# Rotary embedding on one core: three TensorE tiles instead of five, one store on another queue, the first batch's store cut into three

## The chip, the cores and the metric

The kernel runs on one core of a Trainium2 chip. The metric is device microseconds (us) of one execution of the whole program: it loads the input from HBM, rotates it and stores the result to HBM. The core has five engines with an instruction stream each (TensorE, PE in the profile; VectorE, DVE; ScalarE, ACT; GpSimd, POOL; SyncE, SP) and 16 DMA engines that do the transfers. In this kernel DMAs are started from two streams, SP and ACT, and each of the two has a DMA queue of its own: q1 is SP's and q10 is ACT's.

## The reference

`x` is 8 x 2048 x 8 x 64 in float32 (batch, position, head, element); `cos` and `sin` are 2048 x 32. Each half of a head is multiplied with both tables:

```python
x1 = x[..., : x.shape[-1] // 2]
x2 = x[..., x.shape[-1] // 2 :]
out1 = x1 * cos - x2 * sin
out2 = x1 * sin + x2 * cos
return np.concatenate([out1, out2], axis=-1)
```

Input and output are 33.55 MB each, so the work is two products and a sum for each element that is loaded once and stored once.

## The kernel before

**Tiling.** A batch is one tile `xt` of 128 partitions. Partition q holds 16 consecutive positions of 8 x 64 elements, that is 8192 floats, a row of 32 KB that is contiguous in HBM. So a whole batch is moved by one DMA of 128 rows of 32 KB (4 MB), 8 rows for each of the 16 DMA engines. Five such buffers exist (`NBUF`). The result is written over the input in the same tile and stored from there. Batches are numbered 0 to 7 here, as in the code; x3 is the load of batch 3 and s3 its store.

**Loads (SP, line 67).** At the start SP issues the first batch in three pieces of 8, 8 and 16 KB rows (x0), the cosine table after the first of them (line 69), and then x1 to x4. After the work on batch b the loop issues the load of batch b+5 (lines 184 to 193); it takes the buffer of batch b and so waits for that batch's store. These are x5, x6 and x7.

**Units and their three kinds (`rotate`, lines 102 to 168).** A batch is worked on in units of 2048 elements per partition, four to a batch (`UNIT`, 8 KB of a row). The first batch has two half units ahead of three whole ones, the last batch two half units at its end. `kinds` (lines 98 to 100) names those units, always the first of a batch, that do not go the ordinary way. I write (b,u) for unit u of batch b.

- Kind A, the ordinary one: POOL makes the sine product in two halves (line 122, into `t2`), DVE makes the cosine product (line 129, into `t1`, in PSUM, one buffer), and DVE adds the two into `xt` (line 136).
- Kind B: POOL makes the sine product and DVE the cosine product as in A, but TensorE adds them by multiplying both with an identity matrix into PSUM (lines 143 and 144), and ACT copies the sums into `xt` (line 145).
- Kind C: DVE makes both products (lines 129 and 148), TensorE adds them (lines 160 and 161), ACT copies (line 165). POOL does nothing.

So a unit of kind A costs DVE two passes, B one, C two; POOL has two halves to do in A and B, and none in C. Before the change (1,0) and (3,0) are C, (2,0), (4,0) and (5,0) are B, all others A. `t2` of kinds A and B has three buffers, `t1` of kind B and both products of kind C share two others (`t1s`), and the PSUM tile `o` of the sums has one buffer.

**Order.** Nearly all instructions are held in program order on their engine (`keep`). Each engine works through its own list: DVE unit by unit, POOL the same units ahead of it, as far as loads and the three buffers of `t2` allow.

**Stores (line 74).** A store is issued when the units it covers are done. `shares` (lines 177 to 182) gives the cuts: batch 0 in two stores of 16 KB rows, batches 1 to 6 in one store of 32 KB rows, batch 7 in stores of 16, 8 and 8 KB rows. Stores of batches 0 to 6 go out on ACT's stream, in between its copies; those of batch 7 on SP's.

Of the kernel before, what the change touches and what calls it, by code (L numbers as in the profile page):

```python
# [10 lines left out]
def kernel(  # L11
# [7 lines left out]
    nc = tc.nc  # L19
# [4 lines left out]
    B, S, H, D = x.shape  # L24
    Dh = D // 2
    P = 128
    HD = H * D
    R = S // P
    ROW = R * HD
    UNIT = 4 * HD  # L30
    NBUF = 5
    C = 512
    last = B - 1
# [36 lines left out]
        xts[b] = xt  # L70

    def store(b, lo, n):
        queue = nc.sync if b == last else nc.scalar
        keep(queue.dma_start(out=ov[b, :, lo : lo + n], in_=xts[b][:, lo : lo + n]))  # L74

    keep(nc.scalar.dma_start(out=sin_sb, in_=sin_src))
# [19 lines left out]
        return dataclasses.replace(a, ap=[a.ap[0][:], a.ap[1][:], [0, n], a.ap[-1][:]])  # L96

    kinds = {}
    for b, kind in ((1, "C"), (2, "B"), (3, "C"), (4, "B"), (5, "B")):
        kinds[(b, 0)] = kind  # L100

    def rotate(b, lo, n):
# [73 lines left out]

    def shares(b):
        if b == 0:
            return [2 * UNIT, 2 * UNIT]
        if b == last:  # L180
            return [2 * UNIT, UNIT, UNIT]
        return [ROW]

    for b in range(B):
        done = 0
        outs = list(spans(shares(b)))
        for lo, n in spans(pieces(b)):
            rotate(b, lo, n)
            done = lo + n
            while outs and sum(outs[0]) <= done:  # L190
                store(b, *outs.pop(0))
        if b + NBUF <= last:
            load(b + NBUF)
# [30 lines left out]
```

## Time and profile before

| what | value |
|---|---|
| three runs | 163.75, 163.81, 164.03 us, median 163.81 us |
| profiled execution | span 161.8 us from its first to its last instruction (161.82 unrounded) |
| DVE busy | 140.1 us, 87% of the span |
| POOL busy | 138.9 us, 86% |
| PE busy | 49.4 us, 31% |
| ACT busy | 12.8 us, 8% |
| time of the DMA packets, as a share of 16 engines' span | 55.5% on q1, 42.6% on q10 |
| HBM read, written | 34.08 MB, 33.55 MB |

The profile has no separate device time for the profiled execution; its span is all that it gives. The runs' median lies 2.0 us above the span, and these 2.0 us are what lies around the first and the last instruction. Times inside the profile count from the span's start. "Busy" counts an engine's own work and not the time in which it waits or issues DMAs. The trace also has a record of each DMA packet, with its queue, start, duration and size. In this kernel a packet is one row of a tile, so that a load of 128 rows is 128 packets, 8 for each DMA engine.

### The profile page before, as it was taken

The numbers are of one execution on the slowest core, as the hardware profiler recorded it, in microseconds if no ns is written. First come the engines' busy times: TensorE is split into PE (matmuls) and PEld (weight loads), VectorE is DVE, ScalarE is ACT, GpSimd is POOL, SyncE is SP. The second block draws the span as 40 slices with busy tenths as digits, with TensorE's granted clock in tenths as the row PEclk, the third lists the DMA queues.
The fourth block names the chain that finished last, engine by engine and source line by source line (L and its number), as shares of the span: only waits on it lengthen the run. The fifth ranks groups of instructions, "written<-read, shape, count | busy, mean of one in ns | idle before, by whom it ended". The sixth has DMA issues, their size and how long they took to land.

```text
span 161.8 us, 459 instructions
## 1 busy us (share of the span) xinstructions
PE 49.4 (31%) x80; PEld 18.5 (11%) x80; DVE 140.1 (87%) x66; ACT 12.8 (8%) x14; POOL 138.9 (86%) x70
## 2 busy tenths in 40 slices
PE   0000000597309760978049714972000000000000
PEld 0000000142004220322023301330000000000000
DVE  0297999999999999999999999199989999899950
ACT  3300000002200220021000220022000000000000
POOL 1399997998999999992999959999899997999800
PEclk9999999999975998589957995699655555555555
DMA  5999999999999999899899999999999999999995
GB/s 158 425 454 494 413 308 446 413 470 405 462 405 462 389 502 405 389 510 397 389 510 397 389 512 397 397 502 397 397 488 413 405 478 413 405 478 409 397 419 225
DMA packets 3314, 67.65 MB, mean 418 GB/s; under 512 B 368, under 2 KB 368, under 8 KB 624
## 3 DMA queue, kind: packets, MB, share of 16 engines
q1 hardware_dynamic: 2016, 38.01, 55.5%
q10 hardware_dynamic: 1296, 29.62, 42.6%
q14 instruction: 2, 0.02, 0.0%
HBM read 34.08 MB, written 33.55 MB: 418 GB/s over the span
## 4 chain that ended last, share of the span: by engine, by line
DMA 48%; DVE 37%; POOL 9%; issue 2%; DVEq 0%; SPq 0%; POOLq 0%; ACTq 0%
DMA xt<-in_x_dram 26%; DVE t L129 18%; DMA out_dram<-xt 18%; DVE xt L136 17%; POOL t L122 9%; DMA sin_sb<-in_sin_dram 4%; DVE t L148 1%; DVEq L136 0%; SPq L67 0%; POOLq L122 0%; ACTq L74 0%
## 5 line engine op out<-in xcount | busy, mean ns | idle before, releaser
L122 POOL TENSOR_TENSOR t<-xt,sin_sb 128x1024 f32<-128x1024 f32 (+1 forms) x32 | 70.4, 2199 | 13.5 <-DMA xt<-in_x_dram 8.3
L129 DVE TENSOR_TENSOR t<-xt,cos_ps 128x2048 f32<-128x2048 f32 (+1 forms) x34 | 73.4, 2167 | 0.8
L122 POOL TENSOR_TENSOR t<-xt,nsin 128x1024 f32<-128x1024 f32 (+1 forms) x32 | 70.3, 2196 | 0.0
L136 DVE TENSOR_TENSOR xt<-t,t 128x2048 f32<-128x2048 f32 (+1 forms) x29 | 62.2, 2145 | 8.2 <-POOL t L122 5.5
L143 PE MATMUL o<-t,eye 128*128 128x512 f32 x24 | 17.0, 799 | 23.1 <-DVE t L129 19.6
L160 PE MATMUL o<-t,eye 128*128 128x512 f32 x16 | 12.0, 844 | 37.8 <-DVE t L129 35.6
L144 PE MATMUL o<-t,eye 128*128 128x512 f32 x24 | 14.9, 709 | 0.0
L145 ACT COPY xt<-o 128x1024 f32<-128x1024 f32 x6 | 6.1, 1012 | 45.7 <-PE o L144 45.7
L143 PEld LDWEIGHTS o<-t,eye 128*128 128x128 f32 x24 | 5.5, 256 | 32.5 <-issue 26.5
L160 PEld LDWEIGHTS o<-t,eye 128*128 128x128 f32 x16 | 3.7, 256 | 43.2 <-issue 39.4
L165 ACT COPY xt<-o 128x1024 f32<-128x1024 f32 x4 | 4.0, 1012 | 47.8 <-PE o L161 47.8
L93 DVE COPY cos_ps<-cos_sb 128x512 f32<-128x512 f32 x1 | 0.7, 695 | 6.9 <-DMA cos_sb<-in_cos_dram 6.9
L144 PEld LDWEIGHTS o<-t,eye 128*128 128x128 f32 x24 | 5.6, 234 | 8.2 <-issue 7.6
L161 PE MATMUL o<-t,neye 128*128 128x512 f32 x8 | 6.3, 875 | 0.2
L148 DVE TENSOR_TENSOR t<-xt,sin_ps 128x2048 f32<-128x2048 f32 x2 | 4.6, 2281 | 0.0
L161 PE MATMUL o<-t,eye 128*128 128x512 f32 x8 | 4.1, 592 | 0.0
L161 PEld LDWEIGHTS o<-t,neye 128*128 128x128 f32 x8 | 2.2, 300 | 5.3 <-issue 3.6
L161 PEld LDWEIGHTS o<-t,eye 128*128 128x128 f32 x8 | 1.5, 190 | 1.9 <-issue 1.9
L90 ACT ACT_TABLE_LOAD x1 | 1.3, 1283 | 1.2 <-PEq L208 1.2
L90 ACT ACTIVATE nsin<-sin_sb 128x512 f32<-128x512 f32 x1 | 0.6, 629 | 4.0 <-DMA sin_sb<-in_sin_dram 4.0
L91 ACT COPY sin_ps<-sin_sb 128x512 f32<-128x512 f32 x1 | 0.6, 580 | 0.0
L80 POOL MEMSET eye<- 128x128 f32 x1 | 0.2, 204 | 0.3 <-POOLq L208 0.3
(6 smaller groups left out, 1.0 us busy)
## 6 DMA issues: line engine op xcount, KB each, us to landing
xt<-in_x_dram SPq DMA_DIRECT2D x7, 4096.0 KB, 42.8
out_dram<-xt ACTq DMA_DIRECT2D x6, 4096.0 KB, 27.2
out_dram<-xt ACTq DMA_DIRECT2D x2, 2048.0 KB, 22.3
xt<-in_x_dram SPq DMA_DIRECT2D x2, 1024.0 KB, 6.7
xt<-in_x_dram SPq DMA_DIRECT2D x1, 2048.0 KB, 12.2
out_dram<-xt SPq DMA_DIRECT2D x1, 2048.0 KB, 9.9
out_dram<-xt SPq DMA_DIRECT2D x2, 1024.0 KB, 6.2
sin_sb<-in_sin_dram ACTq DMA_DIRECT2D x1, 256.0 KB, 5.7
```

The costliest lines, as they stand in the source:

```text
L90: keep(nc.scalar.mul(nsin, sin_sb, -1.0))
L93: keep(nc.vector.tensor_copy(cos_ps, cos_sb))
L122: nc.gpsimd.tensor_mul(out=t2u[:, :, u, :].rearrange("p (r h) d -> p r h d", h=H), in0=xu[:, :, 1 - u, :].rearrange("p (r h) d -> p r h d" ...
L129: nc.vector.tensor_mul(out=t1.rearrange("p (r k d) -> p r k d", r=nr, d=Dh), in0=xk, in1=rep(cos_ps[:, r0 : r0 + nr, :], 2 * H),)
L136: keep(nc.vector.tensor_add(out=xt, in0=t1, in1=t2))
L143: nc.tensor.matmul(oc, eye, t1[:, cs], start=True, stop=False)
L144: nc.tensor.matmul(oc, eye, t2[:, cs], start=False, stop=True)
L145: keep(nc.scalar.copy(xt[:, 2 * j * C : 2 * (j + 1) * C], o))
L148: nc.vector.tensor_mul(out=t2.rearrange("p (r k d) -> p r k d", r=nr, d=Dh), in0=xk, in1=rep(sin_ps[:, r0 : r0 + nr, :], 2 * H),)
L160: nc.tensor.matmul(oc, eye, t1u[:, gs, u, :], start=True, stop=False)
L161: nc.tensor.matmul(oc, eye if u else neye, t2u[:, gs, 1 - u, :], start=False, stop=True)
L165: nc.scalar.copy(xu[:, :, u, :], o.rearrange("p (g d) -> p g d", d=Dh))
```

## The change

Three edits, and nothing else:

```diff
     def store(b, lo, n):
-        queue = nc.sync if b == last else nc.scalar
+        queue = nc.sync if b in (last, B - NBUF) else nc.scalar
         keep(queue.dma_start(out=ov[b, :, lo : lo + n], in_=xts[b][:, lo : lo + n]))
...
-    for b, kind in ((1, "C"), (2, "B"), (3, "C"), (4, "B"), (5, "B")):
+    for b, kind in ((1, "B"), (3, "C"), (5, "B")):
         kinds[(b, 0)] = kind
...
         if b == 0:
-            return [2 * UNIT, 2 * UNIT]
+            return [2 * HD, UNIT + 2 * HD, 2 * UNIT]
```

The first edit puts s3 (batch 3 = `B - NBUF`) on SP's stream. In program order the last load, x7, is issued right after batch 2, so s3 stands behind x7 on SP and on q1. The second makes (1,0) a B where it was a C, and (2,0) and (4,0) ordinary A units; (3,0) stays C and (5,0) stays B. The third cuts the store of batch 0 into rows of 4, 12 and 16 KB: the first part can go out when the first half unit is done, the second after the third piece, the last after the fifth.

## The prediction

> **What bounds the kernel now.** I began with the page's head, slices and queues.
>
> ```profile
> span 161.8 us, 459 instructions
> ...
> DMA  5999999999999999899899999999999999999995
> ...
> q1 hardware_dynamic: 2016, 38.01, 55.5%
> q10 hardware_dynamic: 1296, 29.62, 42.6%
> ```
>
> The packets of both queues fill 98.1% of 16 engines' span. By the packet records the first packet starts at 1.76 us and the last ends at 160.55; the packets' durations sum to 158.68 us per engine. So the DMA engines are never idle between their first and last packet, and no edit here takes a byte away. Next, the two busy engines' waits and DVE's timeline:
>
> ```profile
> POOL t L122 <- DMA xt<-in_x_dram: 8.3, 6, 3.0
> ...
> DVE xt L136 <- POOL t L122: 5.5, 4, 3.6
> ```
>
> ```profile
> 27.69 2.28 DVE L129 TENSOR_TENSOR t<-xt,cos_ps 128x2048 f32<-128x2048 f32 x1
> 29.88 2.28 DVE L148 TENSOR_TENSOR t<-xt,sin_ps 128x2048 f32<-128x2048 f32 x1
> 32.08 2.29 DVE L129 TENSOR_TENSOR t<-xt,cos_ps 128x2048 f32<-128x2048 f32 x1
> 34.48 2.29 DVE L136 TENSOR_TENSOR xt<-t,t 128x2048 f32<-128x2048 f32 x1
> 36.80 2.30 DVE L129 TENSOR_TENSOR t<-xt,cos_ps 128x2048 f32<-128x2048 f32 x1
> ...
> 105.13 2.29 DVE L136 TENSOR_TENSOR xt<-t,t 128x2048 f32<-128x2048 f32 x1 [3.57 <-POOL t L122]
> ...
> 119.66 2.29 DVE L136 TENSOR_TENSOR xt<-t,t 128x2048 f32<-128x2048 f32 x1 [0.46 <-POOL t L122]
> ...
> 139.09 2.29 DVE L136 TENSOR_TENSOR xt<-t,t 128x2048 f32<-128x2048 f32 x1 [0.64 <-POOL t L122]
> ...
> 154.79 1.23 DVE L136 TENSOR_TENSOR xt<-t,t 128x1024 f32<-128x1024 f32 x1
> ```
>
> DVE runs back to back; its waits for POOL are 5.5 us in four places. It ends at 156.02, the last 1 MB store is issued, its first packet starts at 157.43, just as the 8 KB store before it drains (last packet 157.73). So two bounds meet at the end: DMA work and the DVE chain. Less DVE work gains nothing, more is paid.
>
> **What a unit costs DVE.** From starts in the rows above: A is 4.72 us (32.08 to 36.80), C is 4.39 (27.69 to 32.08). B is one pass, 2.19 (the spacing of the passes at 27.69 and 29.88). An A directly before a B or C is 4.61 (57.77 to 62.38). A unit's second pass starts 2.40 after its first. POOL's half unit takes 2.29 to the next one, a unit 4.58.
>
> **Edit 1, three TensorE tiles.** (1,0) turns from C to B: DVE loses 2.20 and POOL gains 4.58 there. (2,0) and (4,0) turn from B to A: each costs DVE 4.72 - 2.19, and 0.11 because the A before loses its short end, 2.64. POOL's work there is unchanged. PE loses 32 of its 80 matmuls, and ACT four copies of 1.01; both engines wait most of the time, so this is worth nothing.
>
> The first cost is where POOL is late:
>
> ```profile
> 26.04 2.33 POOL L122 TENSOR_TENSOR t<-xt,sin_sb 128x1024 f32<-128x1024 f32 x1 [0.93 <-DMA xt<-in_x_dram]
> ...
> 32.92 2.33 POOL L122 TENSOR_TENSOR t<-xt,nsin 128x1024 f32<-128x1024 f32 x1
> ```
>
> POOL starts batch 1 when x1 lands, S = 26.04. Its first four halves end at 35.25. Before, these were (1,1) and (1,2), and C kept DVE busy meanwhile. After, they are (1,0) and (1,1). DVE would be ready to add (1,1) at 27.69 + 2.19 + 2.40 = 32.28, but can start only at S + 9.24. From there DVE has 4.72 per unit against POOL's 4.58 and stays the later one.
>
> From the add of (1,1) to DVE's end before: 156.02 - 34.48 = 121.54. Subtract the three waits above, less the ordinary gap of 0.10 in each: 3.46 + 0.36 + 0.53 = 4.35. They go because DVE arrives later than POOL: DVE starts batch 5 at about 103 instead of 97.07, while x5 need not be later. Add 2 x 2.64 = 5.28. The chain is **122.47 us**, and DVE ends at S + 9.24 + 122.47 = S + 131.71. With S = 26.04 that is 157.75, already 1.73 later than now.
>
> A new wait must be ruled out: `t2` has three buffers, and a B holds its buffer until TensorE has read it. Before, PE read (2,0)'s until 59.3 and POOL started (2,3) at 54.36 without a wait, in another buffer. If (1,3) should get (1,0)'s buffer, PE (10.8 us per B tile, from about 30.1) frees it at 40.9; POOL wants it at S + 13.7. That costs 0 to 1 us, and nothing from S = 27.2 on.
>
> **Edit 3, the first store in three.** Packet durations are 0.084 us for 2 KB, 0.309 for 8, 0.611 for 16, 1.213 for 32. In a straight line a row of 4 KB is 0.16 and one of 12 KB 0.46, an estimate from these. Batch 0's store is then 8 x (0.16 + 0.46 + 0.61) = 9.84 per engine against 9.78: nothing. But it starts earlier. The first part is ready at 10.26 (DVE's first add ends there), 8 us before the present first store, and ACT has nothing else to do. Its packets alternate row for row with x0's and x1's: x2 beside 16 KB rows took 14.1 us, near 8 x (1.213 + 0.611); x5 beside 32 KB rows 18.4, near 16 x 1.213. So all 8 of its rows go ahead of x1's end (1.27 us), and, since the second part is ready at 18.36 and queued behind, 0 to 3 rows of 12 KB (I take 1.5, 0.69). Now 0.76 us of store packets per engine go ahead of it. x1 lands 1.20 later.
>
> Against this stands a slow stretch:
>
> ```profile
> 20.00:24.00 4.00, 0.00 (x0) 0.00 (x0) 3.86 (x3) 0.00 (x0) 4.00 (x3) 1.00 0.91 303
> 24.00:94.00 70.00, 39.59 (x64) 14.77 (x64) 68.48 (x31) 7.30 (x8) 65.34 (x29) 0.85 1.00 432
> ```
>
> The last column is GB/s. x1's rows took up to 2.09 us there, 0.84 us per engine in excess, while nothing was stored; with the first store packets it ends. Whether stores in between prevent it no row says: 0 to 0.84, I take half. S = 26.04 + 1.20 - 0.42 = 26.82, with ends 25.71 (no 12 KB row, no slow stretch) and 27.93 (three rows, all of it).
>
> **Edit 2, s3 on SP.** On SP it is queued behind x7, whose issue waits for s2 (at 91.4 now); behind it stand only batch 7's stores from about 148. No load waits for s3, since batch 8 does not exist. After s2 the ACT queue is empty until s4 is ready near 104, so x6 and x7 get all engines (9.7 us per batch instead of 18.4). x7 lands near 115 instead of 134.3; s3 follows beside s4. That removes POOL's waits for x6 and x7 (0.76 and 1.14), but DVE is by then 2.5 us later than now and would not have felt them. Worth 0. DMA stays fed: without s5 its work lasts to about 131, and s5 is ready near 120.
>
> **The sum.** DVE ends at 26.82 + 131.71 = 158.5, against 156.02. From there to the span's end it is 5.8 us now; I take 5.6, because the last store no longer meets the one before it (some engines finished it 0.5 late), bounds 5.3 to 5.8. By then the other DMA work is done (160.5 less the last store's 2.5 is 158.0, and its first packet needs 1.4 from issue). Span 164.1; with the 2.0 that the median lies above the span, **166.1 us**, 1.4% slower. Own range: 25.71 + 131.71 + 5.3 + 2.0 = 164.7, and 27.93 + 131.71 + 5.8 + 2.0 = 167.4.
>
> **Rivals.**
> - *DMA stays the bound*: the wait at (1,1) fails to appear or is taken back, so that DVE ends at 156.02 + 5.28 - 2.20 - 4.35 = 154.8 and the last packet still ends at 160.55: 163.8. For it speaks the full DMA row; against it that POOL's two units after x1 need 9.2 us whoever waits. The Trainium skill ("DMA: Bandwidth & Descriptors", Where 436 GB/s comes from) puts the fabric's ceiling at 435.2 GB/s; the 432 above agrees with it, and by that rule alone the time would not move. 7%.
> - *Faster*: the slow stretch between 20 and 24 us is a matter of reading only, and the early 4 KB rows end it. DMA work is then 0.84 shorter: 163.0. It decides only if DVE ends before about 155.2, so it needs the first rival's condition too. 3%.
> - *A held buffer*: POOL's (5,3) gets the `t2` buffer of (5,0). PE then frees it only near 118, POOL ends at 122.8, and DVE, ready near 119, waits 3.7 more: 169.8. None of the three B tiles before did it. 5%.
> - *A queue is served in bulk*: an engine takes all 8 rows of a store before it changes queue. Then 8 x (0.16 + 0.46) = 4.96 goes ahead of x1, S is 29.8, the time 169.1. The Trainium skill (the same page, Queues, rings and completion order) says that a DMA engine changes its queue only after a packet, typically of 9 to 17 descriptors. Against it: from 22.7 to 23.2 us sixteen rows of x1 start between the first and the second row of the first store. 3%.
>
> **Chances.** The forecast 82%, the rivals as given. A measurement of this kernel can tell about 0.2%, 0.33 us, from no change. Slower: 82 + 5 + 3 = 90%; same 7%; faster 3%. The range 164.7 to 167.4 is the forecast's own, which its unknown costs make, and leaves the rivals' 18% out.
>
> **What will show it.** Right: DVE's first wait after 16 us stands at the add of (1,1), near 36, about 3.8 long, and none of the waits at 105, 119 and 139 is left; DVE ends near 158.5; x7 lands before 120; the DMA row has a gap ahead of the last store. Wrong: x1 landing outside 25.7 to 28, a wait of DVE for POOL in batches 5 to 7, or DVE done by 156.

## The result, and the profile after

The changed kernel takes 164.32 us (median of 4 runs, 164.25 to 164.40), the kernel before 163.78 (4 runs, among them the three listed above). The ratio is **1.0038, with a 95% interval of 1.0024 to 1.0052**: slower by 0.54 us. The direction is the forecast's. The size is not: 2.3 us were forecast, and 164.32 lies below the range of 164.7 to 167.4. The profiled execution of the changed kernel took 164.31 us, 1.8 more than its span.

The same rows of the page as before:

```profile
span 162.5 us, 388 instructions
...
DMA  5999999899999999999989999999999999999966
...
q1 hardware_dynamic: 2160, 42.21, 61.1%
q10 hardware_dynamic: 1296, 25.43, 36.6%
```

The last two slices of the DMA row read 66 where they read 95. The engines now run dry once, near the end. s3 shows in the queues: 4 MB have gone from q10 to q1. By the packet records x7's last packet ends at 116.9 us (132.6 before) and x7 lands at 118.6 (134.3), so s3's place did what it should.

DVE's waits and its own timeline (start, duration, engine, line, operation; in brackets the idle time ahead of it and what ended it):

```profile
DVE xt L136 <- POOL t L122: 3.7, 2, 2.9
```

```profile
27.89 4.48 DVE L129 TENSOR_TENSOR t<-xt,cos_ps 128x2048 f32<-128x2048 f32 x2
35.24 2.29 DVE L136 TENSOR_TENSOR xt<-t,t 128x2048 f32<-128x2048 f32 x1 [2.87 <-POOL t L122]
37.57 2.29 DVE L129 TENSOR_TENSOR t<-xt,cos_ps 128x2048 f32<-128x2048 f32 x1
...
107.72 2.29 DVE L136 TENSOR_TENSOR xt<-t,t 128x2048 f32<-128x2048 f32 x1
...
122.00 2.29 DVE L136 TENSOR_TENSOR xt<-t,t 128x2048 f32<-128x2048 f32 x1 [0.20 <-DVE t L129]
...
140.89 2.29 DVE L136 TENSOR_TENSOR xt<-t,t 128x2048 f32<-128x2048 f32 x1
...
156.59 1.23 DVE L136 TENSOR_TENSOR xt<-t,t 128x1024 f32<-128x1024 f32 x1
```

The new wait stands at the add of (1,1), as forecast; the three later ones (now at the rows of 107.72, 122.00 and 140.89) are gone or down to 0.20. DVE ends at 157.82, 1.80 later than before. POOL's first unit of batch 1 starts where it did before:

```profile
26.04 2.32 POOL L122 TENSOR_TENSOR t<-xt,sin_sb 128x1024 f32<-128x1024 f32 x1 [0.70 <-DMA xt<-in_x_dram]
```

So S is 26.04, and S plus the forecast's 131.71 gives 157.75 against the measured 157.82. The chain of DVE was right to 0.07 us. What lies behind it was not. These are the DMA engines from 156 to 160 us (each row of a tile counts in the slice in which it starts), first of the kernel before, then of the changed one: 40 slices of 0.1 us, and the one DMA issued in this window with its median time from issue to landing.

```profile
DMA  7999599599799599599599399379579579779322
...
out_dram<-xt SPq DMA_DIRECT2D x1, 1024.0 KB, 4.9
```

```profile
DMA  5995995992790590020000000099199359519709
...
out_dram<-xt SPq DMA_DIRECT2D x1, 1024.0 KB, 3.9
```

Before, the last store is issued at 156.05 into a queue that is still busy with the one before it, and takes 4.9 us to land. After, it is issued at 157.84, when hardly a row is left to start (one slice of 2 at 157.7, zeros from 157.8 to 158.6), and takes 3.9. DVE's end came 1.8 later, the end of the program 0.7.

### The profile page after: what moved, and what is told of

The parts are those of the page before. It is cut to its first block, busy times and chain, and to the rows that moved or that the text cites. A ratio compares the mean times of both kernels' runs of the same rounds, so it can differ in the third digit from the quotient of the medians.

```text
span 162.5 us, 388 instructions
## 1 busy us (share of the span) xinstructions
PE 30.9 (19%) x48; PEld 11.6 (7%) x48; DVE 142.9 (88%) x67; ACT 8.7 (5%) x10; POOL 143.2 (88%) x72
## 5 line engine op out<-in xcount | busy, mean ns | idle before, releaser
L122 POOL TENSOR_TENSOR t<-xt,sin_sb 128x1024 f32<-128x1024 f32 (+1 forms) x33 | 73.0, 2211 | 8.0 <-DMA sin_sb<-in_sin_dram 5.4
L122 POOL TENSOR_TENSOR t<-xt,nsin 128x1024 f32<-128x1024 f32 (+1 forms) x33 | 73.0, 2211 | 0.0
L136 DVE TENSOR_TENSOR xt<-t,t 128x2048 f32<-128x2048 f32 (+1 forms) x31 | 66.8, 2154 | 6.8 <-POOL t L122 3.7
L143 PE MATMUL o<-t,eye 128*128 128x512 f32 x16 | 12.2, 856 | 58.5 <-DVE t L129 56.2
L160 PE MATMUL o<-t,eye 128*128 128x512 f32 x8 | 6.0, 846 | 27.5 <-DVE t L129 26.4
L144 PE MATMUL o<-t,eye 128*128 128x512 f32 x16 | 10.6, 749 | 0.0
L143 PEld LDWEIGHTS o<-t,eye 128*128 128x128 f32 x16 | 3.7, 256 | 64.3 <-issue 60.0
L145 ACT COPY xt<-o 128x1024 f32<-128x1024 f32 x4 | 4.0, 1012 | 68.0 <-PE o L144 68.0
L144 PEld LDWEIGHTS o<-t,eye 128*128 128x128 f32 x16 | 4.2, 264 | 6.0 <-issue 6.0
L160 PEld LDWEIGHTS o<-t,eye 128*128 128x128 f32 x8 | 1.9, 257 | 30.7 <-issue 28.7
L165 ACT COPY xt<-o 128x1024 f32<-128x1024 f32 x2 | 2.0, 1012 | 35.9 <-PE o L161 35.9
L161 PE MATMUL o<-t,neye 128*128 128x512 f32 x4 | 3.1, 867 | 0.1
L148 DVE TENSOR_TENSOR t<-xt,sin_ps 128x2048 f32<-128x2048 f32 x1 | 2.3, 2280 | 0.0
L161 PE MATMUL o<-t,eye 128*128 128x512 f32 x4 | 2.0, 592 | 0.0
L161 PEld LDWEIGHTS o<-t,neye 128*128 128x128 f32 x4 | 1.0, 289 | 2.6 <-DVE t L148 1.6
L161 PEld LDWEIGHTS o<-t,eye 128*128 128x128 f32 x4 | 0.8, 190 | 1.0 <-issue 1.0
```

The costliest lines, as they stand in the source:

```text
L122: nc.gpsimd.tensor_mul(out=t2u[:, :, u, :].rearrange("p (r h) d -> p r h d", h=H), in0=xu[:, :, 1 - u, :].rearrange("p (r h) d -> p r h d" ...
L136: keep(nc.vector.tensor_add(out=xt, in0=t1, in1=t2))
L143: nc.tensor.matmul(oc, eye, t1[:, cs], start=True, stop=False)
L144: nc.tensor.matmul(oc, eye, t2[:, cs], start=False, stop=True)
L145: keep(nc.scalar.copy(xt[:, 2 * j * C : 2 * (j + 1) * C], o))
L148: nc.vector.tensor_mul(out=t2.rearrange("p (r k d) -> p r k d", r=nr, d=Dh), in0=xk, in1=rep(sin_ps[:, r0 : r0 + nr, :], 2 * H),)
```

## The experiments

The edits are numbered as in the prediction: edit 1 changes the kinds, edit 2 the queue of s3, edit 3 the cut of the first store. Ratios are against the kernel before, measured beside each experiment, where its median was 163.62 or 163.63 us.

**Theory 1**: two bounds, of which the later counts. DMA work ends the span near 161.8 whatever DVE does; DVE's end plus the last store on an idle queue, about 4.7 us, is the other. Before the change DVE had some 1.1 us of slack. **Theory 2** is the forecast's: the end follows DVE from the first microsecond, by 5.3 to 5.8 us, and something else in the change took time back. **Theory 3**: the cost comes from the new rows or the new queue, not from the kinds.

### Each edit alone

`kinds_only`, edit 1 alone:

```diff
-    for b, kind in ((1, "C"), (2, "B"), (3, "C"), (4, "B"), (5, "B")):
+    for b, kind in ((1, "B"), (3, "C"), (5, "B")):
```

> The kernel before with edit 1 alone: (1,0) as B, (2,0) and (4,0) as A; s3 and the first store as they were. Theory 1 (the end is the later of two bounds, DMA work, which ends the kernel at about 163.8 us, and the end of DVE plus about 4.7 us of last store plus 2.0; so DVE has about 1.1 us of slack before): DVE ends near 157.8, 1.8 later than before, of which 0.7 shows: 164.3 to 164.6 us, the whole of the change's cost. Theory 2 (the forecast's: the end always follows DVE by 5.3 to 5.8 us, and the early 4 KB rows or the moved store take something back): without the two other edits the time is at least 165.2. Theory 3 (the cost comes from the smaller rows or from s3's place, and the kinds are hidden): 163.8.

Measured: 164.47 us, ratio 1.0048 (1.0036 to 1.0060). DVE ends at 157.91, POOL starts batch 1 at 26.13. This lies where theory 1 put it (164.3 to 164.6) and is the change's whole cost, its interval overlapping the change's own; nothing in the two other edits is needed to explain it, and they take back nothing that shows.

`cut_only`, edit 3 alone:

```diff
-            return [2 * UNIT, 2 * UNIT]
+            return [2 * HD, UNIT + 2 * HD, 2 * UNIT]
```

> The kernel before with edit 3 alone: the first batch's store in rows of 4, 12 and 16 KB. Theory 1: DMA work is the same, DVE's end too; 163.6 to 164.0 us, within 0.2% of before. Theory 2: x1 lands up to 0.8 us later and that is made up by DVE's later waits; 163.8 as well, but POOL's first unit of batch 1 starts at 26.5 or later. Theory 3: about 164.3. In the packet records the slow rows of x1 between 20 and 24 us, 0.84 us per engine, are either gone (they belonged to reading alone) or there.

Measured: 163.42 us, 0.9996 (0.9985 to 1.0008). POOL's first unit of batch 1 starts at 26.10: x1 is not late. Its slow rows are gone, but the excess of all packets over the usual (median) duration of their size is 1.62 us per engine, against 1.56 before; it is now spread over many rows from 20 us on. DVE ends at 154.45, 1.6 earlier, where I had expected no change: x5 lands at 93.6 instead of 95.8, and the wait at (5,1) falls from 3.57 to 1.48.

`s3_only`, edit 2 alone:

```diff
-        queue = nc.sync if b == last else nc.scalar
+        queue = nc.sync if b in (last, B - NBUF) else nc.scalar
```

> The kernel before with edit 2 alone: s3 on SP, behind x7. Theories 1 and 2: x6 and x7 land earlier (x7 well before 125 instead of 134), DVE's waits at 119 and 139 us go, DVE ends about 0.9 earlier, and the time stays at 163.8, since DMA work is the bound; within 0.2%. Theory 3: above 164.1, because DMA runs dry somewhere once s3 has left its place.

Measured: 163.74 us, 1.0008 (0.9999 to 1.0018). x7's last packet ends at 123.1 instead of 132.6, and DVE ends at 153.50, 2.5 us earlier than before and more than the 0.9 expected, because the wait at (5,1) falls too, from 3.57 to 1.74 (x5 lands at 92.8 instead of 95.8). The time does not follow. Theory 3 falls with these three runs.

`s3_and_cut`, edits 2 and 3 with the five TensorE tiles (the two diffs above):

> The kernel before with edits 2 and 3 and its own five TensorE tiles. Theory 1: DVE ends near 155, DMA work is the bound: 163.6 to 164.0 us; what the change costs is gone with the kinds. Theory 3: about 164.3, as the whole change. If the slow rows of x1 are gone for good and nothing takes their place, as low as 163.0.

Measured: 163.34 us, 0.9981 (0.9973 to 0.9990). It is the fastest of the family by median together with `late_first` below, and beats both kernels, by 0.3 us against before, which theory 1 did not give (163.6 to 164.0). DVE ends at 154.13.

### How much slack DVE had

A needless copy of a table on DVE, of about 0.70 us, leaves all loads, stores and results as they are and only moves DVE's end. The diff for one copy; the others have `range(2)` and `range(4)`:

```diff
+        if b == last and lo == UNIT:
+            for _ in range(1):
+                keep(nc.vector.tensor_copy(cos_sb, cos_ps))
```

> The kernel before with one needless copy on DVE (cos_ps back into cos_sb, which no one reads any more, about 0.70 us) ahead of (7,1). Output unchanged. It delays DVE's end by 0.7 us and nothing else. Theory 1 (1.1 us of slack ahead of the DMA bound): no change, 163.6 to 164.0. Theory 2 (the end follows DVE): plus 0.6 to 0.7, 164.4.

> The kernel before with two such copies on DVE ahead of (7,1), about 1.4 us. Theory 1: 1.4 less 1.1 of slack, plus 0.3: 164.1. Theory 2: plus 1.2 to 1.4, 165.1.

> The kernel before with four such copies on DVE ahead of (7,1), about 2.8 us. Theory 1: 2.8 less 1.1, plus 1.7: 165.5, and DVE's end to the span's end is 4.7 us instead of 5.8. Theory 2: plus 2.6 to 2.8, 166.5, with 5.3 to 5.8 from DVE's end to the span's end.

Measured: one copy 163.56 us, 0.9999 (0.9990 to 1.0008); two copies 163.69, 1.0003 (0.9995 to 1.0012); four copies 165.12, 1.0083 (1.0069 to 1.0096). Of the first 1.4 us at most 0.2 shows, and the next 1.4 cost 1.4. With 1.1 us of slack theory 1 gave 164.1 for two copies and 165.5 for four; both came out 0.4 lower, so in these runs the slack was nearer 1.4. It differs between executions: DVE's end less the copies is 155.6 in the profile of `delay1` and 156.0 in those of the two others. Two rows of DVE in the kernel with four copies, the copies and the last pass:

```profile
141.47 2.86 DVE L130 COPY cos_sb<-cos_ps 128x512 f32<-128x512 f32 x4
...
157.61 1.23 DVE L139 TENSOR_TENSOR xt<-t,t 128x1024 f32<-128x1024 f32 x1
```

DVE ends at 158.84 and the span at 163.6, 4.8 later (line 136 of the kernel before is line 139 here). The last store shows the same two things as in the changed kernel, here from 157 to 161 us, again 0.1 us a slice: a hole in the DMA row and a short landing.

```profile
DMA  9999599597390340000000000019509709909909
...
out_dram<-xt SPq DMA_DIRECT2D x1, 1024.0 KB, 3.8
```

No change of kinds, rows or queues is in this kernel, so hole and short landing come from DVE's lateness alone. Theory 2, with 166.5 and a tail of 5.3 to 5.8, falls.

The packet records of all the kernels say what the last store waits for. In the nine kernels where DVE ends at 156.3 or earlier, its first packet starts at 157.2 to 157.4, whether it was issued at 153.5 or at 156.3: just before the store ahead of it on the same queue drains (157.5 to 157.8). In the five where DVE ends later, it starts 0.85 to 0.86 after DVE's end.

### Giving back one tile, and the two halves of edit 1

`after_b4`, the changed kernel with one of the two B tiles again:

```diff
-    for b, kind in ((1, "B"), (3, "C"), (5, "B")):
+    for b, kind in ((1, "B"), (3, "C"), (4, "B"), (5, "B")):
```

> The changed kernel with (4,0) given back to TensorE as kind B: DVE has 2.64 us less to do than in the changed kernel and ends near 155.2. Theory 1: the DMA bound decides again, 163.6 to 164.0 us, 0.3 to 0.7 less than the changed kernel and not 2.6. Theory 3: the time stays with the changed kernel's, 164.3.

Measured: 163.73 us, 1.0005 (0.9996 to 1.0013) against before. DVE ends at 156.29, 1.5 earlier than in the changed kernel and not 2.6, since a wait for POOL (0.94 at 106.19) and one of 0.53 came back. Giving back one tile removes the whole cost.

`c_to_b` and `b_to_a`, the two halves of edit 1 on the kernel before:

```diff
-    for b, kind in ((1, "C"), (2, "B"), (3, "C"), (4, "B"), (5, "B")):
+    for b, kind in ((1, "B"), (2, "B"), (3, "C"), (4, "B"), (5, "B")):
...
-    for b, kind in ((1, "C"), (2, "B"), (3, "C"), (4, "B"), (5, "B")):
+    for b, kind in ((1, "C"), (3, "C"), (5, "B")):
```

> The kernel before with (1,0) as B instead of C, and the four other TensorE tiles as they were. Theory 1: DVE waits about 3 us for POOL at the add of (1,1), is 0.8 us behind from there, and that delay goes into the wait at (5,1), which shrinks from 3.57 to about 2.7; DVE ends at 156.0 as before, and the time is 163.6 to 164.0. Theory 2 (each edit's cost reaches the end by itself): plus 0.8, 164.5.

> The kernel before with (2,0) and (4,0) as A instead of B, and (1,0) still C. Theory 1: DVE has 5.28 us more to do, its later waits for POOL (4.35 in all) shrink to about nothing, it ends near 156.9, still inside the 1.1 us of slack, and the time is 163.6 to 164.0. So neither half of edit 1 shows by itself, and only both together do (164.47 measured). Theory 2: plus 0.9 at the least, 164.5 to 164.8.

Measured: `c_to_b` 163.72 us, 1.0000 (0.9992 to 1.0009). `b_to_a` 164.03, 1.0023 (1.0014 to 1.0031), a little above what I expected of theory 1 and well below theory 2. In `c_to_b` DVE has two new long waits for POOL, at the adds of (1,1) and (2,1):

```profile
35.29 2.29 DVE L136 TENSOR_TENSOR xt<-t,t 128x2048 f32<-128x2048 f32 x1 [3.10 <-POOL t L122]
...
53.62 2.29 DVE L136 TENSOR_TENSOR xt<-t,t 128x2048 f32<-128x2048 f32 x1 [2.18 <-POOL t L122]
```

They came out of a wait that DVE had anyway: the one at (5,1) is 0.34 instead of 3.57 (I had expected 2.7, and no wait at (2,1)), and DVE ends at 155.41. In `b_to_a` DVE ends at 157.35, 0.4 later than I had worked out; 0.72 of that kernel's DVE time are two short waits (0.52 at 91.03, 0.20 at 121.53) that the profile puts down to DVE itself. DVE's end is then just past the slack, and the time just above the one that DMA work sets. So neither half of edit 1 costs what the whole does.

### The slow rows of x1

The forecast left open whether the slow rows from 20 to 24 us belong to reading alone. `late_first` stores the first batch in one piece:

```diff
-            return [2 * UNIT, 2 * UNIT]
+            return [ROW]
```

> The kernel before with the first batch's store in one piece of 32 KB rows, issued only when the whole batch is done, near 28 us, so that the DMA engines read alone until about 31 us instead of 22. If the slow rows of 20 to 24 us are a matter of reading alone for long, they go on until 31 us, and the packets' excess over their shortest durations grows from 1.56 us per engine to 2.5 or more. If they are tied to that time or to those rows of x1, the excess stays at about 1.5. The time by theory 1: DMA work of the first case plus 1, 164.6; of the second 163.6 to 164.0.

Measured: 163.33 us, 0.9984 (0.9974 to 0.9993), below both expectations. The excess of the packets is 1.60 us per engine, as in the second, but the stretch has moved, which neither foresaw. The stages of the DMA (start and end of a stage, its length, the busy times of the engines, PE's clock, DMA share, GB/s), first of the kernel before, whose row from 20 to 24 us (303 GB/s) the prediction shows, then of this one:

```profile
29.00:33.00 4.00, 2.74 (x3) 1.00 (x4) 4.00 (x3) 0.00 (x0) 4.00 (x3) 1.00 1.10 475
```

```profile
20.00:24.00 4.00, 0.00 (x0) 0.00 (x0) 3.86 (x3) 0.00 (x0) 4.00 (x3) 1.00 0.93 401
...
29.00:33.00 4.00, 2.61 (x3) 1.00 (x4) 4.00 (x3) 0.00 (x0) 4.00 (x3) 1.00 1.09 377
```

A stage of 4 us counts whole rows, so its GB/s swings with the rows that begin in it; the packet records say the same more sharply: the excess is 0.82 us per engine from 20 to 30 us and none from 30 to 40 before, 0.18 and 0.73 here. The slow rows go with the first large store: they begin 1.1 to 1.2 us after its issue (18.36 and 19.5 before, 27.93 and 29.2 here) and stand ahead of and around its first packets (22.2 before, 32.3 here). They last about as long and cost as much, in a profile that is of this kernel's longest run. Reading alone for longer did not make more of them.

`s3_late` adds edit 2 to that:

```diff
-        queue = nc.sync if b == last else nc.scalar
+        queue = nc.sync if b in (last, B - NBUF) else nc.scalar
...
-            return [2 * UNIT, 2 * UNIT]
+            return [ROW]
```

> The kernel before with its five TensorE tiles, s3 on SP behind x7, and the first batch's store in one piece of 32 KB rows. Theory 1: DMA work decides, with DVE done near 154. The first store in one piece measured 163.33 and s3 with the cut store 163.34, both 0.3 under before; if each of these comes from DMA work that went away, the two together stay at that floor, 163.2 to 163.4; if they add, 163.0; if they were chance, 163.6. In the packet records the slow rows stand once more just ahead of the first store's packets, near 30 us, with about 0.8 us per engine in excess.

Measured: 163.60 us, 0.9996 (0.9987 to 1.0005). The slow rows stand near 31 us again (0.60 us per engine). The 0.3 us of `late_first` did not come back with s3 moved as well, as expected if they were chance, though the intervals of `late_first` and `s3_and_cut` each leave out 1. What makes these two 0.3 faster stays open: the profile of `s3_and_cut` has 0.18 us per engine less excess than before (1.38), and that of `late_first` is of its longest run.

### All kernels by their two bounds

DVE's end and the span are those of each kernel's profiled execution; the last column is the median of its runs. The profiled executions of `c_to_b` (163.89), `late_first` (164.22), `delay2` (163.95) and `delay4` (165.42) were the longest of their runs, those of `delay1` (163.48) and `b_to_a` (163.89) the shortest. The 163.78 of the kernel before is from the result above; beside the experiments it took 163.62 or 163.63.

| kernel | DVE ends | span | span less DVE's end | runs |
|---|---|---|---|---|
| s3_only | 153.50 | 161.9 | 8.4 | 163.74 |
| s3_late | 153.62 | 161.8 | 8.2 | 163.60 |
| s3_and_cut | 154.13 | 161.7 | 7.6 | 163.34 |
| cut_only | 154.45 | 161.6 | 7.2 | 163.42 |
| c_to_b | 155.41 | 162.1 | 6.7 | 163.72 |
| late_first | 155.78 | 162.4 | 6.6 | 163.33 |
| before | 156.02 | 161.8 | 5.8 | 163.78 |
| after_b4 | 156.29 | 161.7 | 5.4 | 163.73 |
| delay1 | 156.32 | 161.7 | 5.4 | 163.56 |
| b_to_a | 157.35 | 162.1 | 4.8 | 164.03 |
| delay2 | 157.41 | 162.2 | 4.8 | 163.69 |
| the changed kernel | 157.82 | 162.5 | 4.7 | 164.32 |
| kinds_only | 157.91 | 162.7 | 4.8 | 164.47 |
| delay4 | 158.84 | 163.6 | 4.8 | 165.12 |

Down to `delay1` the span is 161.6 to 162.4 wherever DVE ends. From `b_to_a` on it is DVE's end plus 4.7 to 4.8. The two lines cross near 157, 1.0 us behind DVE's end in the profile of the kernel before: the slack. By the medians of the delayed kernels it is nearer 1.4.

## Why the prediction was right in direction and wrong in size

- *What bounds the kernel.* Right that DMA packets fill the span and that less DVE work gains nothing (`s3_only` and `cut_only`: DVE ends 1.6 to 2.5 earlier, with no gain clear of noise). **Wrong that "more is paid"** from the first microsecond. The two bounds did not meet: 1.0 us lay between them in the profile, and of 1.4 us of added DVE work at most 0.2 showed.
- *Edit 1.* Right in each term: the add of (1,1) starts at 35.24, where S + 9.24 gives 35.28 (its wait is 2.87 and not 3.8, because S was smaller than forecast), the three later waits vanish, and S to DVE's end is 131.78 against 131.71 forecast. `kinds_only` shows it to be the whole cost.
- *Edit 3.* The step "x1 lands 1.20 later", less half a slow stretch, S = 26.82, failed by 0.78. All eight 4 KB rows went ahead of x1's end, as forecast, but no 12 KB row did (the first starts at 24.91), and x1's own slow rows went altogether (its rows average 1.217 us, 1.318 before). What happened is near the lower end of that step's bounds, 25.71, and 0.2 of the rest is that the whole start ran later in this execution (POOL's first product at 6.74 instead of 6.53). The cause that I weighed was not the right one either: reading alone is not what makes the slow rows. Nor did they end "with the first store packets": of the 0.84 us per engine 0.45 is in rows of x1 that start after the first of these, at 22.2.
- *Edit 2.* Right: worth nothing. x7 lands at 118.6 ("x7 lands near 115"), and no wait of DVE for x6 or x7 is left.
- *The sum.* **The step that failed most is "From there to the span's end it is 5.8 us now; I take 5.6 ... bounds 5.3 to 5.8".** It is 4.7. I read the 1.4 us from the last store's issue to its first packet as the price of issuing; it was the wait for the 8 KB store ahead on the same queue. On an idle queue the first packet starts 0.83 us after the issue (158.67 and 157.84 in the changed kernel). The tail fell by 1.08 in all: 0.55 is this wait, 0.45 is that the store's packets take 2.67 us from the first start to the last end instead of 3.12, with no other store beside them, and the rest comes after the last packet. I had even written that the last store would no longer meet the one before it, and allowed 0.2 for that.
- Together: 0.71 less at DVE's end (158.53 to 157.82) and 0.9 less behind it make the 1.6 us between the forecast span of 164.1 and the measured 162.5; another 0.2 is the time around the span, 1.8 in this execution instead of 2.0. The 2.0 was a median less the span of another execution; in every execution that lists both it is 1.7 to 1.9.
- *The rivals.* None happened. The first store's rows did alternate with x1's (13.9 to 24.8 us), so no queue was served in bulk. POOL's (5,3) did wait 1.69 us for a buffer (at 110.09), but for DVE's add of (5,1) and not for PE, and nothing came of it.

## What to carry to other kernels

Where two bounds seem to meet at the end, measure the slack between them before a cost is summed: put known amounts of needless work on one engine and see from which amount the time moves, over several runs, since the slack itself differs between executions. A tail that is read off a profile belongs to the bound that was active there; once the other bound decides, the same store finds an idle queue and the tail is another. Costs of two edits to the same engine do not add if each fits into a wait or a slack of its own: the halves of this edit cost 0 and 0.2%, the whole 0.5%.

## What the runs showed of the hardware that was not expected

- From a DMA's issue to its landing, 1 MB to HBM took 4.9 us behind another store on the same queue, and 3.8 to 3.9 on idle engines (window views above).
- Some 0.6 to 0.9 us per engine of slow load rows follow the issue of the first large store, at 20 to 25 us or at 29 to 33, wherever that store is. With a first store of 4 KB rows they are spread thin over later rows, and the sum nearly stays (1.55 us per engine in the changed kernel, 1.62 in `cut_only` and 1.38 in `s3_and_cut`, 1.56 before). Why is open.
- A B tile's held `t2` buffer does make POOL wait in two of the kernels (2.13 us in `s3_and_cut`, 1.25 in `after_b4`, both at (5,0) for PE's work on (4,0)). Neither is slower than the kernel before.
